# The sums of the up-projection's weights: made on GpSimd in the mLSTM heads, kept in DRAM, loaded as weight tiles

## The chip, the core and the metric

The program runs on one core of one Trainium2 chip. The metric is device time in microseconds (us), the median of several executions. The engines are named as in the profile: PE is TensorE (matmuls), PEld its weight loads, DVE is VectorE, ACT is ScalarE, POOL is GpSimd, and SP is SyncE, whose queue issues the DMAs of this kernel. Each engine, SP too, takes its instructions strictly in the order in which the program has them.

## What is computed

One layer of a decoder in float32, for 1024 prompt rows and 8 × 8 sample rows: an input projection, four retention heads and four mLSTM heads, an output projection, and a feed-forward part with a causal convolution of width 3:

```python
h = rmsnorm(x, pre_mix_g)
proj = (h @ w_in).astype(f32)                       # 1024 -> 4 x 512 + 4 x 512 + 8
ret_out, S_new = retention_chunked(q_r, k_r, v_r, S_ret)
ml_out, C_new, n_new, m_new = mlstm_chunked(q_m, k_m * scale, v_m, i_pre, f_pre, C, n, m)
...
x = x + rmsnorm(mix, post_mix_g)
h2 = rmsnorm(x, pre_ffn_g)
up = h2 @ w_up                                      # 1024 -> 2 x 2816
padded = jnp.concatenate([conv_buf, up], axis=1)
conv = sum(padded[:, j:j + L] * conv_w[j] for j in range(CONV_W)) + conv_b
gate, val = conv[..., :D_FF], conv[..., D_FF:]
ffn = (gelu(gate) * val) @ w_down                   # 2816 -> 1024
x = x + rmsnorm(ffn, post_ffn_g)
```

## The kernel before

**Products.** Every float32 operand of a matmul is split into a high and a low part (ACT copies the high part, DVE subtracts it from the operand to get the low one, `split_to`, L145 and L147), and each product is three matmuls: high × high, high × low, low × high. The 1088 rows stand in four blocks of 272 columns, so that a matmul of the projections is 128 × 128 weights on 272 columns.

**Stages.** Loads and the first norm (to about 50 us of the profiled execution); the retention heads r0 to r3 (to 295); the mLSTM heads m0 to m3 (to 515); the output projection (to about 650); the norm behind it, together with the first two column tiles of the up-projection in plain form (`PLAIN` = 2; to 712); the other 20 column tiles j = 2 to 21 (to about 1152); the down-projection and the last norm.

**A head** (`mix_head`, L468) has five turns (L662): two pairs of 128-row chunks, the sample rows, two more pairs. Before each turn `front` projects the inputs of the next one. The weights `st_in` are loaded by SP (L133, two buffers) and split. For the sample rows GpSimd makes `vx` (L613) and scales the old state `sb` by `dec` (L616, mLSTM heads only); PE multiplies `vx` (`us`, L621), DVE adds (L624), and the state is stored (L627) and the next head's loaded into the same single buffer (L502). On GpSimd there is nothing else in the mLSTM heads. At the end of each turn `next(rows, None)` takes one step of a generator, which is in use during the retention heads alone.

**The up-projection.** A column tile j is a pair of 128 columns, one of the gate and one of the value. Its four 128 × 512 weight blocks A11, A12, A21, A22 (the inner dimension in two halves, gate and value) are not multiplied as they are: with sums of them (Strassen's scheme, in Winograd's form) there are seven products of half the inner dimension for two blocks of rows instead of eight. `weight_prep(j)` loads two 512 KB tiles `st_up` (L133), GpSimd makes the four sums in place (L859, L865 to L867: 128 × 512 each), and seven halves of 128 × 512 are split one at a time on ACT and DVE. A j has 7 products × 2 row blocks × 12 matmuls = 168 matmuls (L928 to L930); DVE adds what comes out of PSUM (L902, L906), and DVE and ACT make the convolution (L941, L943, L948), GELU and the product of the two (L950), GpSimd the sums of those for the down-projection (L958).

**Order.** The Tile framework orders the instructions of each engine ahead of time with a model of their durations; the result is one fixed list for each engine. All DMAs stand in SP's one list. A DMA that waits for its data (a store that waits for GpSimd) holds up all that stand behind it there.

**Memory.** `tok` (L226) hands out 128 × 1088 tiles in turn from seven buffers; two of them are taken at the start by the rotary tables `rot`, which are last used in the retention heads.

Of the kernel before, what the change touches and what calls it, by code (L numbers as in the profile page):

```python
# [23 lines left out]
T = LP + TS  # L24
# [7 lines left out]
JT = DFF // P  # L32
# [5 lines left out]
PLAIN = 2  # L38
# [54 lines left out]
def hybrid_layer_kernel(ctx: ExitStack, tc: tile.TileContext, a: dict, o: dict):  # L93
    nc = tc.nc
# [9 lines left out]
    last = {}  # L104
# [4 lines left out]
    dr = pool("dr", bufs=1, space=bass.MemoryType.DRAM)  # L109
# [21 lines left out]
    def stage_w(src, name):  # L131
        st = wp.tile([P, 2 * HB], F32, tag="wst", name=f"st_{name}")[:, :D]
        nc.sync.dma_start(st, src)  # L133
        return st
# [7 lines left out]
    def split_to(x, hi, lo, eng=nc.vector, after=None):  # L142
        act, dve = after or (None, None)
        with tc.issue_after(act.ins) if act else nullcontext():
            nc.scalar.activation(hi, x, AF.Copy)  # L145
        with tc.issue_after(dve.ins) if dve and eng is nc.vector else nullcontext():
            eng.tensor_tensor(lo, x, hi.bitcast(F32), ALU.subtract)  # L147
        return hi, lo
# [69 lines left out]
    mpool = lambda name, **k: mixctx.enter_context(tc.tile_pool(name=name, **k))  # L218
    mp = mpool("mp", bufs=1)
    cst = mp.tile([P, C_N], F32, name="cst")  # L220
    rb = mp.tile([P, T], F32, name="rb")
    ident = cst[:, C_ID:C_ID + P]
    tokp = mpool("tokp", bufs=7)
    m2 = mpool("m2", bufs=2)

    def tok(name, rows=P, dt=F32):  # L226
        return tokp.tile([P, T], dt, tag="tok", name=name)[:rows, :]
# [1 line left out]

    h = []  # L230
    xs = [flat("x", b, k=KT) for b in range(4)]
    rot = [tok(f"rot{i}") for i in range(2)]
    nc.sync.dma_start(vec, a["vec"])
    first = (2 * NH, 2 * NH + 1)
    staged = [stage_w(a["wi"][first[0]], f"in{first[0]}")]
# [12 lines left out]
    sums = [m2.tile([P, NB, 129], F32, tag=t, bufs=1, name=f"sums_{t}").rearrange("p s v -> p (s v)") for t in ("vx", "sb")]  # L248
    sqs = [m2.tile([P, Q], F32, tag="sw", name=f"sq{i}") for i in range(2)]
    for b in range(4):  # L250
        n = BLK[b][1]
# [57 lines left out]
    cols = mp.tile([P, 9, 3 * NH], F32, name="cols")  # L309
# [158 lines left out]
    def mix_head(hd, ml):  # L468
# [207 lines left out]
        nc.sync.dma_start(o["cp" if ml else "sp"][hd], S)  # L676
        todo()

    rows = iter(())
    for hd in range(NH):  # L680
        mix_head(hd, False)
        if hd == 0:
            gate_proj()
            rows = gate_rows()
    for _ in rows:
        pass
    for hd in range(NH):
        mix_head(hd, True)

    mx = []  # L690

# [28 lines left out]
    fp = pool("fp", bufs=2)  # L720
# [4 lines left out]
    def wtile():  # L725

        wtag[0] += 1
        return (wp, "w") if wtag[0] % 4 in (1, 2) else (fp, "d")
# [102 lines left out]
    acc = out_proj(0)  # L831
    acc = out_proj(1, spaced(post_mix(0, acc)))
    acc = out_proj(2, spaced(post_mix(1, acc)) + [lambda: first_half(0)])
    acc = out_proj(3, spaced(post_mix(2, acc)) + [lambda: first_half(1)])
# [5 lines left out]

    def weight_prep(j):

        h0, h1 = slice(0, D // 2), slice(D // 2, D)
        s0, s1 = stage_w(a["wu"][j, 0], f"up{j}_0"), stage_w(a["wu"][j, 1], f"up{j}_1")
        a11, a12, a22, a21 = s0[:, h0], s0[:, h1], s1[:, h0], s1[:, h1]
        plain = j < PLAIN
        t1 = None if plain else fp.tile([P, D // 2], F32, tag="s1", bufs=1, name=f"s1_{j}")
        ws = {}

        def parts(i, eng=nc.vector, **src):  # L850
            p, tag = wtile()
            hi = p.tile([P, D], F32R, tag=tag + "hi", name=f"wh_up{j}_{i}")
            lo = p.tile([P, D], F32R, tag=tag + "lo", name=f"wl_up{j}_{i}")
            for (name, x), c in zip(src.items(), (h0, h1)):
                ws[name] = split_to(x, hi[:, c], lo[:, c], eng, (last["sq"], last["acc"]) if i in (1, 2) else None)

        e = nc.gpsimd
        if not plain:
            e.tensor_tensor(t1, a21, a22, ALU.add)  # L859
        parts(0, A11=a11, A12=a12)  # L860
        if plain:
            parts(3, A22=a22, A21=a21)
            yield ws
            return
        e.tensor_tensor(a21, a11, a21, ALU.subtract)  # L865
        e.tensor_tensor(a11, t1, a11, ALU.subtract)  # L866
        e.tensor_tensor(a12, a12, a11, ALU.subtract)  # L867
        yield ws
        parts(1, S2=a11, S1=t1)
        yield  # L870
        parts(2, S4=a12, S3=a21)
        yield
        parts(3, A22=a22)
        yield

    def half(U, th, i):
# [101 lines left out]
    sums = {"T1": mo[0][0], "T3": mo[0][1], "T2": mo[1][1]}  # L978
    firsts = []

    def begin_plain(j):
        ws = next(weight_prep(j))
        firsts.append((j, ws, up_products(j, ws)[1]()))
# [139 lines left out]
    acc = [t_acc[b // 2][:, b % 2 * Q:(b % 2 + 1) * Q] for b in range(4)]  # L1123
# [172 lines left out]
```

## Time and profile before

| | before |
|---|---|
| median of 3 runs | 1428.85 us (1427.64 to 1430.25) |
| the profiled execution, own time | 1428.44 us |
| its span from first to last instruction | 1426.7 us |
| PE busy | 1361.6 us (95%) |
| DVE busy | 1060.2 us (74%) |
| ACT busy | 587.0 us (41%) |
| POOL busy | 436.4 us (31%) |
| bytes moved by DMA | 135.12 MB, 95 GB/s over the span |
| mean granted TensorE clock | 0.985 of full speed |

The busy time of an engine is the time in which one of its instructions ran, waits left out. PE is busy nearly everywhere, so the first question to each part of the kernel is how many of its matmuls ran in how much time; the matmuls' own durations overlap (a matmul of 272 columns is shown with some 290 ns, while they follow each other every 125 ns).

### The profile page before, as it was taken

The page shows a single profiled execution, that of the slowest core. Times are in us where ns is not written, and L with a number is a line of the kernel's source. Part 1 is how long each engine was busy: PE and PEld are TensorE (multiplying, and loading weights), DVE is VectorE, ACT ScalarE, POOL GpSimd, SP SyncE. Part 2 cuts the span into 40 slices and gives each one's busy share as a digit, 9 for nine tenths or more (in the row PEclk, how much of TensorE's full clock was granted, in tenths as well). Part 3 has the DMA queues.
Part 4 walks back from the last instruction along what each step waited for, and adds up shares of the span by engine and source line. Part 5 has one row for each costly group of instructions (what it writes and reads, how often), then busy time and mean ns, then how long its engine had stood idle before and what let it go on. Part 6 is the DMA issues. An engine that isn't in the chain of part 4 may idle for free. (4 is left out here: it accounts for less than half of the span.)

```text
span 1426.7 us, 26779 instructions
## 1 busy us (share of the span) xinstructions
PE 1361.6 (95%) x10575; PEld 1332.3 (93%) x10575; DVE 1060.2 (74%) x2064; ACT 587.0 (41%) x1162; POOL 436.4 (31%) x433
## 2 busy tenths in 40 slices
PE   7999999999999999999998999999999979999993
PEld 7899999999999998999998999999999979999993
DVE  7845875455455466568899999999989995995577
ACT  6423542323223236445553433433433444454462
POOL 5200000001001000004456466465465460952015
PEclk9999999999999999999999999999999989999997
DMA  6112111121121113323022223322223394333352
GB/s 233 60 45 73 41 59 54 53 62 48 45 62 47 45 47 112 113 63 122 32 92 87 89 88 112 107 85 84 99 85 115 116 404 121 95 91 93 97 197 114
DMA packets 64478, 135.12 MB, mean 95 GB/s; under 512 B 6112, under 2 KB 30688, under 8 KB 63840
## 3 DMA queue, kind: packets, MB, share of 16 engines
q1 hardware_dynamic: 64352, 133.41, 27.6%
q8 instruction: 83, 1.36, 0.4%
q14 instruction: 43, 0.35, 0.1%
HBM read 97.88 MB, written 35.50 MB: 93 GB/s over the span
## 5 line engine op out<-in xcount | busy, mean ns | idle before, releaser
L159 PE MATMUL in<-hh,wh_in 128*128 128x272 f32 x1024 | 301.8, 295 | 11.1 <-ACT hh L198 6.8
L161 PE MATMUL in<-hh,wl_in 128*128 128x272 f32 x1024 | 301.1, 294 | 1.1 <-DVE wl_in L147 1.1
L160 PE MATMUL in<-hl,wh_in 128*128 128x272 f32 x1024 | 299.8, 293 | 1.2 <-DVE hl L199 1.2
L159 PEld LDWEIGHTS in<-hh,wh_in 128*128 128x128 f32 x1024 | 195.4, 191 | 12.9 <-ACT hh L198 6.8
L161 PEld LDWEIGHTS in<-hh,wl_in 128*128 128x128 f32 x1024 | 194.9, 190 | 3.7 <-issue 2.1
L160 PEld LDWEIGHTS in<-hl,wh_in 128*128 128x128 f32 x1024 | 195.4, 191 | 2.4 <-DVE hl L199 1.5
L147 DVE TENSOR_TENSOR wl_up<-st_up,wh_up 128x512 fp32r<-128x512 f32 x128 | 125.4, 985 | 9.5 <-ACT wh_up L145 9.4
L145 ACT ACTIVATE wh_up<-st_up 128x512 fp32r<-128x512 f32 x128 | 75.1, 620 | 133.1 <-POOL st_up L866 120.4
L1054 DVE TENSOR_TENSOR rb<-rb 128x544 fp32r<-128x544 f32 x78 | 73.1, 949 | 42.4 <-ACT rb L1053 42.2
L943 DVE SCALAR_TENSOR_TENSOR c<-Ug,vec,c 128x1024 f32<-128x1024 f32 x88 | 79.4, 939 | 9.5 <-ACT c L941 9.5
L1074 POOL TENSOR_TENSOR wd<-wd 128x512 f32<-128x512 f32 x44 | 72.0, 1667 | 42.7 <-DVE ra_dhi L1054 33.1
L943 DVE SCALAR_TENSOR_TENSOR c<-Uv,vec,c 128x1024 f32<-128x1024 f32 (+1 forms) x88 | 71.9, 822 | 9.3 <-ACT c L941 9.3
L958 POOL TENSOR_TENSOR act<-act 128x544 f32<-128x544 f32 x44 | 72.4, 1645 | 14.7 <-DVE act L950 10.3
L1053 ACT ACTIVATE rb<-rb 128x544 fp32r<-128x544 f32 x78 | 49.8, 648 | 64.3 <-DMA rb<-bd 58.4
L613 POOL TENSOR_TENSOR vx_r<-vts,cst 64x1024 f32<-64x1024 f32 x4 | 7.6, 1901 | 191.8 <-ACT vts L527 191.8
L902 DVE TENSOR_TENSOR Uv<-Uv,up_S 128x272 f32<-128x272 f32 (+1 forms) x200 | 63.5, 369 | 0.0
L941 ACT ACTIVATE c<-Ug,vec 128x1024 f32<-128x1024 f32 (+1 forms) x44 | 34.6, 835 | 67.0 <-DVE Ug L906 59.3
L145 ACT ACTIVATE wh_in<-st_in 128x1024 fp32r<-128x1024 f32 x32 | 33.9, 1059 | 62.3 <-PE in L160 58.3
L893 POOL MEMSET Ug<- 128x2 f32 x22 | 2.2, 100 | 176.9 <-DVE xr L791 82.1
L859 POOL TENSOR_TENSOR s<-st_up 128x512 f32<-128x512 f32 x20 | 29.0, 1450 | 85.2 <-DMA st_up<-in_wu 82.1
L613 POOL TENSOR_TENSOR vx_m<-vts,cst 64x1032 f32<-64x1032 f32 x4 | 7.7, 1914 | 152.6 <-DVE pt_m L559 152.6
L928 PE MATMUL up_A<-T4h,wh_up 128*128 128x272 f32 x160 | 47.9, 299 | 4.8 <-DVE Uv L902 4.7
(547 smaller groups left out, 4825.1 us busy)
## 6 DMA issues: line engine op xcount, KB each, us to landing
st_up<-in_wu SPq DMA_DIRECT2D x44, 512.0 KB, 3.3
rb<-bd SPq DMA_DIRECT2D x76, 272.0 KB, 2.8
bd<-act SPq DMA_DIRECT2D x33, 544.0 KB, 2.7
st_in<-in_wi SPq DMA_DIRECT2D x32, 512.0 KB, 3.3
wd<-in_wd SPq DMA_DIRECT2D x22, 512.0 KB, 9.3
x<-in_x SPq DMA_DIRECT2D x16, 272.0 KB, 7.0
xr<-in_x SPq DMA_DIRECT2D x8, 544.0 KB, 3.7
x1d<-mo SPq DMA_DIRECT2D x8, 544.0 KB, 3.1
```

The lines of the kernel that those rows point to most:

```text
L145: nc.scalar.activation(hi, x, AF.Copy)
L147: eng.tensor_tensor(lo, x, hi.bitcast(F32), ALU.subtract)
L159: nc.tensor.matmul(ps, hi[:, ws], xh, start=k == 0, stop=False)
L160: nc.tensor.matmul(ps, hi[:, ws], xl, start=False, stop=False)
L161: nc.tensor.matmul(ps, lo[:, ws], xh, start=False, stop=k == KT - 1)
L902: nc.vector.tensor_tensor(o_, o_ if x is None else c(x), c(ps), ALU.add)
L928: nc.tensor.matmul(ps, wh[:, c], xh[:, k, n], start=k == 0, stop=False)
L943: nc.vector.scalar_tensor_tensor(c, u(i), cw(i), c, ALU.mult, ALU.add)
L958: nc.gpsimd.tensor_tensor(o_, x, y, ALU.subtract)
L1053: nc.scalar.activation(hi, x, AF.Copy)
L1054: nc.vector.tensor_tensor(lo, x, hi.bitcast(F32), ALU.subtract)
L1074: nc.gpsimd.tensor_tensor(quad(p, out), quad(p, x), quad(p, y), op)
```

## The change

For j = 2 to 21 the sums of the weights are no longer made in the up-projection. During the four mLSTM heads a new generator `weight_sums` takes the weights in 40 pieces: two pieces c = 0, 1 for each j, one j for each of the 5 × 4 turns. For a piece SP loads 256 columns of each of the four blocks in two DMAs of 256 KB (128 × 2 × 256 elements each), GpSimd makes the four sums in place (128 × 256 each), and SP stores the 512 KB tile with S2, S1, S4, S3 to a tensor `sd` in DRAM. In the up-projection `weight_prep` then loads, for each j, the 512 KB tile of A11 and A12, two 512 KB tiles from `sd`, and the 256 KB of A22 alone; it splits three times 128 × 1024 and once 128 × 512, in place of seven times 128 × 512, and GpSimd makes no sums there.

The pieces lie in the two tiles that held `rot` (one buffer for each c); for that, `rot` has tiles of its own, and `tok` has five buffers in place of seven.

```diff
-    tokp = mpool("tokp", bufs=7)
+    tokp = mpool("tokp", bufs=5)
...
-    rot = [tok(f"rot{i}") for i in range(2)]
+    rot = [mp.tile([P, T], F32, tag=f"rot{i}", name=f"rot{i}") for i in range(2)]
...
+    sd = dr.tile([JT, P, 4, D // 2], F32, name="sd")
+
+    def weight_sums():
+
+        for j in range(PLAIN, JT):
+            for c in range(2):
+                cols = slice(c * 256, c * 256 + 256)
+                g = mp.tile([P, T], F32, tag=f"rot{c}", name=f"sg{j}_{c}")[:, :D].rearrange("p (b n) -> p b n", b=4)
+                w0, w1 = (a["wu"][j, q].rearrange("p (b n) -> p b n", b=2)[:, :, cols] for q in range(2))
+                nc.sync.dma_start(g[:, 1:3, :], w0)
+                nc.sync.dma_start(g[:, 0::3, :], w1)
+                a22, a11, a12, a21 = (g[:, i, :] for i in range(4))
+                for o_, x, y, op in ((a21, a11, a21, ALU.subtract), (a22, a22, a21, ALU.subtract),
+                                     (a11, a22, a11, ALU.add), (a12, a12, a22, ALU.subtract)):
+                    nc.gpsimd.tensor_tensor(o_, x, y, op)
+                nc.sync.dma_start(sd[j][:, :, cols], g)
+                if c:
+                    yield
+
...
+    rows = weight_sums()
     for hd in range(NH):
         mix_head(hd, True)
+    for _ in rows:
+        pass
...
-        h0, h1 = slice(0, D // 2), slice(D // 2, D)
-        s0, s1 = stage_w(a["wu"][j, 0], f"up{j}_0"), stage_w(a["wu"][j, 1], f"up{j}_1")
-        a11, a12, a22, a21 = s0[:, h0], s0[:, h1], s1[:, h0], s1[:, h1]
...
-        def parts(i, eng=nc.vector, **src):
+        def parts(i, x, *names):
             p, tag = wtile()
-            hi = p.tile([P, D], F32R, tag=tag + "hi", name=f"wh_up{j}_{i}")
-            lo = p.tile([P, D], F32R, tag=tag + "lo", name=f"wl_up{j}_{i}")
-            for (name, x), c in zip(src.items(), (h0, h1)):
-                ws[name] = split_to(x, hi[:, c], lo[:, c], eng, (last["sq"], last["acc"]) if i in (1, 2) else None)
+            n = len(names) * D // 2
+            hi = p.tile([P, D], F32R, tag=tag + "hi", name=f"wh_up{j}_{i}")[:, :n]
+            lo = p.tile([P, D], F32R, tag=tag + "lo", name=f"wl_up{j}_{i}")[:, :n]
+            split_to(x, hi, lo, nc.vector, (last["sq"], last["acc"]) if i in (1, 2) else None)
+            for c, name in enumerate(names):
+                cols = slice(c * D // 2, (c + 1) * D // 2)
+                ws[name] = hi[:, cols], lo[:, cols]
...
-        if not plain:
-            e.tensor_tensor(t1, a21, a22, ALU.add)
-        parts(0, A11=a11, A12=a12)
+        parts(0, stage_w(a["wu"][j, 0], f"up{j}_0"), "A11", "A12")
...
-        e.tensor_tensor(a21, a11, a21, ALU.subtract)
-        e.tensor_tensor(a11, t1, a11, ALU.subtract)
-        e.tensor_tensor(a12, a12, a11, ALU.subtract)
         yield ws
-        parts(1, S2=a11, S1=t1)
-        yield
-        parts(2, S4=a12, S3=a21)
-        yield
-        parts(3, A22=a22)
+        sums = sd[j].rearrange("p b n -> p (b n)")
+        for i, names in ((1, ("S2", "S1")), (2, ("S4", "S3"))):
+            parts(i, stage_w(sums[:, (i - 1) * D:i * D], f"up{j}_{i}"), *names)
+            yield
+        st = fp.tile([P, D // 2], F32, tag="s1", bufs=1, name=f"st_up{j}_3")
+        nc.sync.dma_start(st, a["wu"][j, 1][:, :D // 2])
+        parts(3, st, "A22")
         yield
```

Lines below the diff's first part carry new numbers in the changed kernel: the loads of `weight_sums` are L689 and L690, its sums L694, its store L695; L902 becomes L920, and L943 becomes L961. In rows of the order a DMA is shown with the shape of one side, and the number at the end of a name is the buffer's.

Where the order changes, first on SP, at the passage from head r3 to m0 (`st_in` are weights of the input projection, `out_ss` the store of a retention state, `sb` the load of the next state, `sg` the pieces). Before:

```order
L133 DMA st_in24_3672<-in_wi 128x1024
L133 DMA st_in17_4103<-in_wi 128x1024
L627 DMA out_ss<-sb_r3_3174 1024x1x128
L502 DMA sb_m0_3782<-in_sc 128x8x128
L133 DMA st_in21_4213<-in_wi 128x1024
```

The same place in the changed kernel:

```order
L133 DMA st_in17_4184<-in_wi 128x1024
L689 DMA sg3_1_3921<-in_wu 128x2x256
L690 DMA sg3_1_3921<-in_wu 128x2x256
L695 DMA sd_276<-sg3_0_3913 512x1x256
L689 DMA sg4_0_4015<-in_wu 128x2x256
L695 DMA sd_276<-sg3_1_3921 512x1x256
L690 DMA sg4_0_4015<-in_wu 128x2x256
L627 DMA out_ss<-sb_r3_3175 1024x1x128
L689 DMA sg4_1_4023<-in_wu 128x2x256
L690 DMA sg4_1_4023<-in_wu 128x2x256
L502 DMA sb_m0_3783<-in_sc 128x8x128
L695 DMA sd_276<-sg4_0_4015 512x1x256
```

So loads and stores of the pieces stand between the loads that the heads need, and each store waits in that list for GpSimd. On GpSimd, the sample rows of head m0, before:

```order
L506 COPY sb_m0_3782<-sn_m0_3784 128x8
L613 TENSOR_TENSOR vx_m0_3938<-vts1_267,cst_81 64x1032
L616 TENSOR_TENSOR sb_m0_3782<-sb_m0_3782,dec_m0_3787 128x1032
L629 COPY sn_m0_3784<-sb_m0_3782 128x8
L506 COPY sb_m1_4433<-sn_m1_4435 128x8
```

And there in the changed kernel:

```order
L694 TENSOR_TENSOR sg7_0_4590<-sg7_0_4590 128x256 x4
L694 TENSOR_TENSOR sg7_1_4598<-sg7_1_4598 128x256 x4
L613 TENSOR_TENSOR vx_m0_3971<-vts1_267,cst_81 64x1032
L694 TENSOR_TENSOR sg8_0_4644<-sg8_0_4644 128x256 x2
L694 TENSOR_TENSOR sg8_1_4652<-sg8_1_4652 128x256
L694 TENSOR_TENSOR sg8_0_4644<-sg8_0_4644 128x256 x2
L694 TENSOR_TENSOR sg8_1_4652<-sg8_1_4652 128x256
L616 TENSOR_TENSOR sb_m0_3783<-sb_m0_3783,dec_m0_3788 128x1032
L694 TENSOR_TENSOR sg8_1_4652<-sg8_1_4652 128x256 x2
L629 COPY sn_m0_3785<-sb_m0_3783 128x8
```

`vx` of m0 now stands behind all sums up to j = 7, and each of these waits for its piece's loads. The third place is DVE in the up-projection, tile j = 15 (`up15_...` are products in PSUM, `c3` the convolution, `wl_up16` low parts of the next tile's weights). Before:

```order
L902 TENSOR_TENSOR Uv15_11666<-Uv15_11666,up15_S31_11847 128x208
L902 TENSOR_TENSOR Uv15_11666<-Uv15_11666,up15_S31_11847 128x8x8
L902 TENSOR_TENSOR Uv15_11666<-Uv15_11666,up15_S31_11847 128x272
L147 TENSOR_TENSOR wl_up16_2_11864<-st_up16_0_11725,wh_up16_2_11863 128x512
L943 SCALAR_TENSOR_TENSOR c3_8292<-Ug15_11663,vec_67,c3_8292 128x1024
L943 SCALAR_TENSOR_TENSOR c3_8292<-Ug15_11663,vec_67,c3_8292 128x64
L147 TENSOR_TENSOR wl_up16_2_11864<-st_up16_1_11727,wh_up16_2_11863 128x512
L902 TENSOR_TENSOR Uv15_11666<-Uv15_11666,up15_A220_11869 128x272
```

In the changed kernel:

```order
L920 TENSOR_TENSOR Uv15_11881<-Uv15_11881,up15_S31_12053 128x208
L920 TENSOR_TENSOR Uv15_11881<-Uv15_11881,up15_S31_12053 128x8x8
L920 TENSOR_TENSOR Uv15_11881<-Uv15_11881,up15_S31_12053 128x272
L961 SCALAR_TENSOR_TENSOR c3_8598<-Ug15_11878,vec_67,c3_8598 128x1024
L961 SCALAR_TENSOR_TENSOR c3_8598<-Ug15_11878,vec_67,c3_8598 128x64
L147 TENSOR_TENSOR wl_up16_2_12072<-st_up16_2_12069,wh_up16_2_12071 128x1024
L920 TENSOR_TENSOR Uv15_11881<-Uv15_11881,up15_A220_12075 128x272
```

Two splits of 512 columns around the convolution have become one of 1024 behind it; the evacuations and the convolution keep their places. The order on PE is the same but for some matmuls of head m1.

More of the change, by code (lines that the diff above doesn't have):

```diff
@@ L841, in weight_prep @@
     def weight_prep(j):
-        h0, h1 = slice(0, D // 2), slice(D // 2, D)
-        s0, s1 = stage_w(a["wu"][j, 0], f"up{j}_0"), stage_w(a["wu"][j, 1], f"up{j}_1")
-        a11, a12, a22, a21 = s0[:, h0], s0[:, h1], s1[:, h0], s1[:, h1]
         plain = j < PLAIN
-        t1 = None if plain else fp.tile([P, D // 2], F32, tag="s1", bufs=1, name=f"s1_{j}")
         ws = {}
-        def parts(i, eng=nc.vector, **src):
+        def parts(i, x, *names):
             p, tag = wtile()
-            hi = p.tile([P, D], F32R, tag=tag + "hi", name=f"wh_up{j}_{i}")
-            lo = p.tile([P, D], F32R, tag=tag + "lo", name=f"wl_up{j}_{i}")
-            for (name, x), c in zip(src.items(), (h0, h1)):
-                ws[name] = split_to(x, hi[:, c], lo[:, c], eng, (last["sq"], last["acc"]) if i in (1, 2) else None)
-        e = nc.gpsimd
-        if not plain:
-            e.tensor_tensor(t1, a21, a22, ALU.add)
-        parts(0, A11=a11, A12=a12)
+            n = len(names) * D // 2
[6 more added lines that the diff above has]
+        parts(0, stage_w(a["wu"][j, 0], f"up{j}_0"), "A11", "A12")
         if plain:
-            parts(3, A22=a22, A21=a21)
+            parts(3, stage_w(a["wu"][j, 1], f"up{j}_1"), "A22", "A21")
             yield ws
             return
-        e.tensor_tensor(a21, a11, a21, ALU.subtract)
-        e.tensor_tensor(a11, t1, a11, ALU.subtract)
-        e.tensor_tensor(a12, a12, a11, ALU.subtract)
         yield ws
-        parts(1, S2=a11, S1=t1)
-        yield
-        parts(2, S4=a12, S3=a21)
-        yield
-        parts(3, A22=a22)
+        sums = sd[j].rearrange("p b n -> p (b n)")
[5 more added lines that the diff above has]
+        parts(3, st, "A22")
         yield
```

## Prediction

> **What bounds the kernel now.** First the head of the page: is one engine the bound, and at what clock?
>
> ```profile
> span 1426.7 us, 26779 instructions
> PE 1361.6 (95%) x10575; PEld 1332.3 (93%) x10575; DVE 1060.2 (74%) x2064; ACT 587.0 (41%) x1162; POOL 436.4 (31%) x433
> ...
> PE   7999999999999999999998999999999979999993
> ...
> PEclk9999999999999999999999999999999989999997
> ```
>
> PE is busy in nearly every slice, at 95% of the span, at full clock; the whole remainder is 65 us. So a change that leaves the matmuls alone can only win PE's gaps, and the question is which gaps lie in the two stages that it touches. Next the windows, one for the mLSTM heads, two for the up-projection, one for the down-projection as a yardstick (columns: window, length, busy us and instructions of PE, PEld, DVE, ACT, POOL, then clock, DMA share, GB/s):
>
> ```profile
> 290.00:515.00 225.00, 225.00 (x1788) 216.38 (x1787) 115.44 (x424) 59.33 (x173) 16.86 (x16) 1.00 0.17 52
> 700.00:825.00 125.00, 118.63 (x928) 116.63 (x927) 120.62 (x174) 58.82 (x95) 75.53 (x81) 1.00 0.23 81
> 825.00:1125.00 300.00, 296.79 (x2339) 294.14 (x2338) 277.13 (x457) 121.11 (x195) 166.83 (x195) 1.00 0.26 94
> 1325.00:1350.00 25.00, 25.00 (x202) 25.00 (x201) 15.68 (x28) 10.98 (x19) 0.00 (x0) 1.00 0.34 95
> ```
>
> In the last window matmuls follow one another without a gap: 202 with two cut by its edges, 200 in 25 us, 0.125 us each. By that step the up-projection's windows have matmuls for 928 × 0.125 = 116.0 us of 125 (9.0 lost) and 2339 × 0.125 = 292.4 us of 300 (7.6 lost). DVE is at 96% and 92% there. In the mLSTM heads PE is busy in all of 225 us, and DVE in half of it.
>
> A second count, over all 20 tiles, from the first matmul of product A11 to its last:
>
> ```profile
> L928 PE MATMUL up_A<-B1h,wh_up x160: 283/288/365, 712.3 to 1131.8; 128*128 128x272 f32 x160
> ```
>
> Between 712.3 and 1131.8 lie 19 tiles × 168 matmuls and 21 of the 20th, 3213 × 0.125 = 401.6 us of 419.5: **17.9 us lost**. That is all that this stage has to give. Who loses it, the waits between 715 and 1145 us say (us in total, times, longest):
>
> ```profile
> ACT wh_up L145 <- POOL st_up L866: 120.4, 17, 7.9
> ...
> PEld up_A L928 <- DVE Uv L902: 5.9, 14, 0.7
> ...
> PE up_A L928 <- DVE Uv L902: 4.6, 11, 1.6
> ...
> PE up_S L928 <- DVE Uv L902: 3.5, 5, 1.3
> ```
>
> PE waits for L902, DVE's evacuation of an earlier product, since a new product needs its PSUM bank; it hardly waits for weights. ACT's 120 us wait for GpSimd's sums is cover, not loss: the split weights are still in time. So the loss is DVE's, a nearly full engine with a list that now and then runs late.
>
> **The gain in the up-projection.** DVE's work is made smaller in two ways. What the splits cost now, and what a split twice as wide costs:
>
> ```profile
> L147 DVE TENSOR_TENSOR wl_up<-st_up,wh_up 128x512 fp32r<-128x512 f32 x128 | 125.4, 985 | 9.5 <-ACT wh_up L145 9.4
> L147 DVE TENSOR_TENSOR wl_up<-s,wh_up 128x512 fp32r<-128x512 f32 x20 | 32.0, 1601 | 0.0
> L147 DVE TENSOR_TENSOR wl_in<-st_in,wh_in 128x1024 fp32r<-128x1024 f32 x32 | 39.6, 1237 | 11.9 <-ACT wh_in L145 11.5
> ...
> L147 DVE TENSOR_TENSOR wl_up<-st_up,wh_up x128: 674/683/1779, 647.5 to 1138.4; 128x512 fp32r<-128x512 f32 x128
> ```
>
> Of seven splits a tile has six of the first row and one of the second: 6 × 0.985 + 1.601 = 7.5 us. After the change there are three of 1024 at 1.237 us (third row) and one of 512 at its undisturbed median of 0.683: 4.4 us. **3.1 us a tile** less. A tile takes 419.5 us / (3213 / 168) = 21.9 us, so DVE falls from 92% to (0.92 × 21.9 − 3.1) / 21.9 = 78%.
>
> Why the mean is 0.985 where the median is 0.683: DVE is held by GpSimd. The clearest case lies in the mLSTM heads (timeline: start, duration; then the same line's durations):
>
> ```profile
> 342.15 1.91 POOL L616 TENSOR_TENSOR sb_m<-sb_m,dec_m 128x1032 f32<-128x1032 f32 x1 [4.52 <-PE o_m L608]
> 342.56 1.50 DVE L578 SCALAR_TENSOR_TENSOR den_m0s<-on_m0s 64x1 f32<-64x1 f32 x1
> ...
> L578 DVE SCALAR_TENSOR_TENSOR den_m<-on_m x8: 146/148/149, 339.7 to 515.9; 128x4 f32<-128x4 f32 x8
> ...
> L902 DVE TENSOR_TENSOR Uv<-Uv,up_A x40: 421/426/434, 742.6 to 1164.3; 128x272 f32<-128x272 f32 x40
> ```
>
> An operation of 0.15 us takes 1.50 us and ends with GpSimd's, 344.06 us both. L902, which takes one input from PSUM, is never longer than 0.434 us though GpSimd is busy in half of that stage. So only DVE operations with two SBUF inputs are held; the splits are such, and the sums are what holds them. GpSimd still has L958 and L1074 there, so some holding stays.
>
> Of the 17.9 us I take **13**: nearly all of the second window's 7.6, where a DVE that is 78% full can catch up, and some 5.5 of the rest, where two more conv outputs and the operand sums of the start compete for DVE whatever the weights do. Bounds: 0 (the order of evacuations on DVE is the same, and the wait is set by order, not by load) and 17.9.
>
> The Trainium skill, page "Perfetto Trace Analysis", section "Identifying the Most-Contended Engine", says to judge TensorE's headroom by the weight loads' busy share rather than the matmuls'; here PEld has 294.14 of 300 us, 5.9 lost in place of 7.6, and by it the forecast would be some 2 us later.
>
> ACT goes from 7 halves to 3 wide splits and one half and is far from full; SP has four loads a tile in place of two, 1.75 MB in place of 1 MB in 21.9 us, about 34 GB/s more on 94. The third load comes a product pair ahead of its use by the order, and lands in some 3.3 us: I cost both at nothing. Without that cover a tile would lose about one landing time, 3 us.
>
> **The cost in the mLSTM heads: GpSimd holds DVE.** The sums' price, from the nearest width:
>
> ```profile
> L205 POOL TENSOR_TENSOR sq<-x x28: 636/832/1691, 6.0 to 48.8; 128x272 f32<-128x272 f32 x28
> ...
> L859 POOL TENSOR_TENSOR s<-st_up x20: 1282/1369/2220, 670.0 to 1120.8; 128x512 f32<-128x512 f32 x20
> ```
>
> Undisturbed, 272 columns take 0.636 us and 512 take 1.282, so 256 take some 0.62; I take 0.65, since DVE is half idle here (high end: the median of the crowded first stage, 0.83). 160 × 0.65 = 104 us, in some 240 us: GpSimd is in a sum 43% of the time. A finish of a head's group has seven small DVE operations with two SBUF inputs, of which L578 is one (8 + 4 finishes: 84), and 12 splits of `st_in` come to it: 96. One that comes while a sum runs waits half of it: 96 × 0.43 × 0.32 = 13 us on DVE. DVE is idle half of this stage, and PE waits for nothing in it; only where DVE works without pause, after the sample rows, does this reach PE. I take **3 us**, bounds 0 and 13.
>
> The Trainium skill ("SBUF — State Buffer", "Who interferes with whom") calls this an exclusive lock that the loser waits out entirely; the 1.50 us row agrees with it, and it speaks against moving sums beside the heads. Its exception for operations with one SBUF input is borne out by L902.
>
> **The cost in the mLSTM heads: the loop of a piece.** A piece's buffer is loaded, summed, stored, and only then free. What the trace has for such DMAs (KB each, us to landing):
>
> ```profile
> st_in<-in_wi SPq DMA_DIRECT2D x32, 512.0 KB, 3.3
> ...
> x1d<-mo SPq DMA_DIRECT2D x8, 544.0 KB, 3.1
> ...
> sb_m<-in_sc SPq DMA_DIRECT2D x4, 512.0 KB, 4.2
> out_cs<-sb_m SPq DMA_DIRECT2D x4, 512.0 KB, 3.9
> rb<-bd SPq DMA_DIRECT2D x76, 272.0 KB, 2.8
> ```
>
> Two loads of 256 KB side by side are taken at 3.1 (272 KB: 2.8; 512 KB: 3.3 to 4.2), the store at 3.2 (3.1 to 3.9), the four sums at 2.6, handing over at 0.3: **9.2 us** a loop, at most 4.2 + 3.9 + 4 × 0.83 + 0.3 = 11.7. The time that it has, one turn:
>
> ```profile
> L613 POOL TENSOR_TENSOR vx_m<-vts,cst x4: 1912/1914/1916, 335.7 to 494.9; 64x1032 f32<-64x1032 f32 x4
> ...
> 335.71 1.92 POOL L613 TENSOR_TENSOR vx_m<-vts,cst 64x1032 f32<-64x1032 f32 x1 [39.89 <-DVE pt_m L559]
> ...
> 341.94 1.60 PEld L621 LDWEIGHTS us_m<-vx_m,kz_m 64*128 64x128 f32 x6 [0.17 <-issue]
> ```
>
> (494.9 − 335.7) / 3 / 5 = 10.6 us a turn, of which I leave 0.6 for SP's and GpSimd's other entries: 10. Two buffers run at once, and GpSimd's sums of both, 5.2 us, fit into it. With 9.2 the loop keeps up, `vx` comes in time, and the term is 0. If it fell behind, `vx` (in GpSimd's list behind all sums up to j = 7) would have 341.94 − 337.63 = 4.3 us before PE stands. The 40 stores that wait in SP's list can delay the weights behind them; GpSimd waits 39.9 us ahead of `vx` today, and weights come a whole projection ahead, so this too is 0 as long as the loop keeps up.
>
> **Elsewhere.** `tok` with five buffers and `rot` on its own leave the retention heads the five that they had. The mLSTM heads have five for seven; the order on PE is the same, so 0. The turn to the down-projection at 1140 to 1180 us moves forward as it is.
>
> **Sum.** 1428.4 − 13 + 3 = 1418.4 us for the profiled execution, which is 0.4 under the median of the runs: **1419 us**. Differences within 0.2% (2.9 us) are about what a measurement of this kernel cannot tell from no change.
>
> **The rivals.**
>
> *The loop is too slow* (slower): at C us a loop, 20 turns lose C − 10 each, less the 4.3 us of slack, at `us` on PE behind a late `vx`. For it: sums, loads and stores are chained through one SP list, and 0.8 us is the whole margin. Against it: the rows' middle values give 9.2. At C = 10.7 it eats the 10 us of net gain; at 11.7 it costs 30 us and the kernel takes 1449. Chance 0.20, most of it on the slower side.
>
> *The order on DVE, not its load, makes PE wait* (same): evacuations now stand behind a split of 1.2 us where they stood behind one of 0.68, and the conv operations of 0.9 us stay. For it: PE's single waits are short, up to 1.6 us, as one operation ahead in a list would make them. Against it: DVE at 96% where the loss is larger, 92% where it is smaller. About 4 us would come back: 1428.4 − 4 + 3, on the median 1428. Chance 0.13.
>
> *The whole loss comes back and holding costs nothing*: 1428.4 − 17.9, on the median 1411. Chance 0.05.
>
> **The numbers.** Forecast (1413 to 1424) 0.62. Faster: 0.62 + 0.05 + 0.03 of the second and third rival's edges = 0.70; within 0.2%: 0.12; slower: 0.18. The range goes from the full gain, 1411, to 1434, a loop of about 11 us; it leaves out some 0.15, above.
>
> **What would show it.** The count of matmuls: a tile every 21.2 to 21.4 us in place of 21.9. DVE at some 78% in 825 to 1125 us, wide splits near 1.24 us, PE's waits for L902 (now L920) down by more than half. In the heads: `vx` still 53.0 us apart, and no idle time of PE ahead of `us`; if PE stands there, the loop was too slow and I was wrong on the price of a loop. Small DVE operations of 0.15 us drawn out to 0.3 to 0.75 us in the heads show the holding; if it shows as idle PE of more than 13 us there, that term was wrong. If DVE falls to 78% and PE's waits stay, the second rival was right.

## The result, and the profile after

The changed kernel takes **1448.41 us** (median of 4 runs, 1444.32 to 1450.48) where the one before takes 1428.76: a ratio of 1.0133, 95% interval 1.0109 to 1.0157. It is slower by some 20 us, outside the range given. Its profiled execution has a span of 1446.2 us, 19.5 more than before. The head of its page:

```profile
span 1446.2 us, 26997 instructions
PE 1366.2 (94%) x10575; PEld 1338.0 (93%) x10575; DVE 1010.8 (70%) x2000; ACT 586.6 (41%) x1098; POOL 420.7 (29%) x513
...
PEclk9999999998989898999999999999999999999997
```

The number of matmuls is the same, DVE is busy 49 us less, and yet the time is longer. Four slices of the clock row, all in the mLSTM heads, are down by a tenth; before there were none there. Cut at the first and the last A11 product of the 20 tiles (the row of the first product, here for the changed kernel), the span falls into three parts:

```profile
L946 PE MATMUL up_A<-B1h,wh_up x160: 283/288/291, 756.7 to 1159.9; 128*128 128x272 f32 x160
```

| us | to the first A11 | the 20 tiles | from the last A11 to the end |
|---|---|---|---|
| before | 712.3 | 419.5 | 294.9 |
| changed | 756.7 | 403.2 | 286.3 |
| difference | +44.4 | −16.3 | −8.6 |

So the up-projection did what the change wanted, and better than forecast: 403.2 us for matmuls of 401.6, and DVE down to 79% in this window (237.54 of 300 us), PE without a gap:

```profile
840.00:1140.00 300.00, 300.00 (x2393) 300.00 (x2392) 237.54 (x429) 124.69 (x159) 73.48 (x142) 1.00 0.41 134
```

The 44.4 us come from the heads. The line of `vx` in the changed kernel:

```profile
L613 POOL TENSOR_TENSOR vx_m<-vts,cst x4: 1904/1906/1909, 344.9 to 539.8; 64x1032 f32<-64x1032 f32 x4
```

PE's waits from 270 to 560 us (us in total, times, longest):

```profile
PE us_m L621 <- POOL vx_m L613: 24.2, 4, 10.2
PE s_m L557 <- DVE sb_m L624: 4.9, 2, 3.9
```

`vx` comes 9.2 us late in m0 and 44.9 us late in m3, 65.0 us apart where it was 53.0. PE, which in this window waited 1.3 us before, all of it at the output projection behind the heads, now stands 29.1 us. That is less than 44.4. The rest is the clock, seen first in the windows around the first such wait (after the five engines: granted clock, DMA share, GB/s):

```profile
335.00:345.00 10.00, 4.89 (x41) 4.30 (x40) 8.58 (x32) 2.33 (x9) 5.80 (x9) 1.00 0.74 243
345.00:350.00 5.00, 3.10 (x5) 1.82 (x6) 2.00 (x3) 0.61 (x3) 1.85 (x1) 0.51 0.72 211
350.00:355.00 5.00, 5.00 (x21) 4.37 (x20) 0.00 (x0) 0.00 (x0) 3.67 (x6) 0.50 0.31 104
355.00:360.00 5.00, 4.00 (x34) 3.79 (x33) 2.40 (x9) 1.21 (x3) 4.03 (x5) 0.97 0.36 119
```

PE stands from about 340 to 347 us, and then works at half clock until about 355: 21 matmuls in 5 us where 40 would fit. A wait of 7 us has so cost some 11. In windows of 0.5 us from 270 to 560 us, PE was busy for 35.1 us at a granted clock near 0.5 (none before); the half of it that is lost, some 17 us, with the 29.1 us of waits makes the 44.4 within 3 us. The Trainium skill, page "TensorE: Matmul & The Clock Gate", Part 1 on the clock gate, says that an idle window halves the clock and that sustained work releases it; the granted clock of 0.50 after the wait agrees.

Why `vx` is late, the chain that ends at `vx` of m0 shows (start, duration, what):

```profile
326.95 2.41 POOL sg L694 x2
...
329.38 3.23 DMA sd<-sg
...
332.62 0.54 SPq L689
...
333.27 0.56 SPq L695
...
333.88 4.85 DMA sg<-in_wu
...
338.89 0.73 POOL sg L694
```

Nothing but the loop of the pieces: sums, store, the next load, sums, up to `vx`. Within it stands a foreign entry, L695 at 333.27: between the two loads of a piece, SP issues the *other* piece's store. What the parts cost, first from the page's DMA issues (KB each, us to landing), then from the lines of a piece's two loads and of the sums:

```profile
sg<-in_wu SPq DMA_DIRECT2D x80, 256.0 KB, 3.4
sd<-sg SPq DMA_DIRECT2D x40, 512.0 KB, 4.1
```

```profile
L689 SPq DMA_DIRECT2D sg<-in_wu x40: 539/540/638, 265.3 to 528.9; - x40
...
DMA to landing us min/median/max: 3.0/3.3/5.7
```

```profile
L690 SPq DMA_DIRECT2D sg<-in_wu x40: 600/624/991, 265.9 to 530.2; - x40
...
DMA to landing us min/median/max: 3.2/4.2/6.0
```

```profile
L694 POOL TENSOR_TENSOR sg<-sg x160: 713/733/1722, 270.9 to 539.1; 128x256 f32<-128x256 f32 x160
```

And what SP waited for in the heads:

```profile
SPq L689 <- DMA sd<-sg: 97.5, 37, 5.6
SPq L695 <- POOL sg L694: 59.6, 21, 4.9
```

The 3.4 us of the page is the median of both loads together; the sums wait for the second one (L690), which lands in 4.2. So: the issue of the first load, behind which the second one stands, 0.6; the second one's landing 4.2; handing over 0.3, an estimate; four sums 3.1 (4 × the mean of 0.784); store 4.1. That makes 12.3 us, where 9.2 was taken and 11.7 was the high end. (The expectation for the stores on ACT's queue below counts 3.4 and so has 11.5.) And the loop in fact took more: the list has six tiles ahead of `vx` of m0, begun at 265.3 and done at 344.9, **13.3 us a tile**. To be in time at 335.7 it would have needed 11.7.

### The profile page after: what moved, and what is told of

It reads as the page before. It is cut to its first block, busy times and chain, and to the rows that moved or that the text cites. A ratio compares the mean times of both kernels' runs of the same rounds, so it can differ in the third digit from the quotient of the medians.

```text
span 1446.2 us, 26997 instructions
## 1 busy us (share of the span) xinstructions
PE 1366.2 (94%) x10575; PEld 1338.0 (93%) x10575; DVE 1010.8 (70%) x2000; ACT 586.6 (41%) x1098; POOL 420.7 (29%) x513
## 4 chain that ended last, share of the span: by engine, by line
PE 67%; DMA 13%; DVE 8%; POOL 4%; issue 3%; ACT 2%; SPq 1%; DVEq 0%; POOLq 0%; ACTq 0%
DMA sd<-sg 6%; DMA sg<-in_wu 5%; PE up_S L948 5%; PE up_S L947 5%; PE up_S L946 5%; PE in L161 5%; PE in L159 5%; PE in L160 5%; PE dn L1137 4%; PE dn L1138 4%; PE dn L1136 4%; PE up_A L947 4%; PE up_A L946 4%; PE up_A L948 4%; POOL sg L694 4%
## 5 line engine op out<-in xcount | busy, mean ns | idle before, releaser
L159 PE MATMUL in<-hh,wh_in 128*128 128x272 f32 x1024 | 304.9, 298 | 10.4 <-ACT hh L198 6.0
L161 PE MATMUL in<-hh,wl_in 128*128 128x272 f32 x1024 | 304.6, 298 | 0.9 <-DVE wl_in L147 0.9
L161 PEld LDWEIGHTS in<-hh,wl_in 128*128 128x128 f32 x1024 | 198.3, 194 | 4.7 <-issue 3.4
L694 POOL TENSOR_TENSOR sg<-sg 128x256 f32<-128x256 f32 x160 | 123.1, 784 | 170.3 <-DMA sg<-in_wu 164.4
L145 ACT ACTIVATE wh_up<-st_up 128x1024 fp32r<-128x1024 f32 x84 | 80.5, 958 | 164.5 <-PE up_S L947 98.9
L147 DVE TENSOR_TENSOR wl_up<-st_up,wh_up 128x1024 fp32r<-128x1024 f32 x84 | 96.9, 1154 | 8.4 <-ACT wh_up L145 8.4
L920 DVE TENSOR_TENSOR Uv<-Uv,up_S 128x272 f32<-128x272 f32 (+1 forms) x200 | 66.8, 377 | 45.8 <-PE up_S L948 45.8
L976 POOL TENSOR_TENSOR act<-act 128x544 f32<-128x544 f32 x44 | 69.1, 1571 | 67.3 <-DMA bd<-act 34.5
L961 DVE SCALAR_TENSOR_TENSOR c<-Uv,vec,c 128x1024 f32<-128x1024 f32 (+1 forms) x88 | 72.2, 824 | 8.6 <-ACT c L959 8.6
L961 DVE SCALAR_TENSOR_TENSOR c<-Ug,vec,c 128x1024 f32<-128x1024 f32 x88 | 68.7, 820 | 1.4 <-ACT c L959 1.4
L147 DVE TENSOR_TENSOR wl_in<-st_in,wh_in 128x1024 fp32r<-128x1024 f32 x32 | 43.1, 1346 | 10.3 <-ACT wh_in L145 9.9
L1213 POOL TENSOR_TENSOR facc<-facc,x1r 128x816 f32<-128x816 f32 (+1 forms) x10 | 21.4, 2158 | 91.0 <-DVE facc L1212 85.1
```

Of the source, the lines that this page charges most:

```text
L159: nc.tensor.matmul(ps, hi[:, ws], xh, start=k == 0, stop=False)
L161: nc.tensor.matmul(ps, lo[:, ws], xh, start=False, stop=k == KT - 1)
L694: nc.gpsimd.tensor_tensor(o_, x, y, op)
L961: nc.vector.scalar_tensor_tensor(c, u(i), cw(i), c, ALU.mult, ALU.add)
```

## The experiments

Theory L: the loop's lateness, carried into the heads by `vx`, is the loss. Rivals: H, GpSimd's sums hold DVE; T, the missing token buffers. The table after the experiments has the three parts of every kernel's profiled execution. Where only one time is given, it is a single run; the kernel before, run beside them, took 1425.7 to 1430.7 us.

**The up-projection alone.** `weight_sums` isn't stepped, and the tiles of sums are raw blocks:

```diff
-    rows = weight_sums()
+    rows = iter(())
...
-            parts(i, stage_w(sums[:, (i - 1) * D:i * D], f"up{j}_{i}"), *names)
+            parts(i, stage_w(a["wu"][j, i - 1], f"up{j}_{i}"), *names)
```

> The sums are not made at all: the heads run without the pieces, and the up-projection loads raw weight blocks of the same size in the place of the stored sums, so its result is another one. Every theory: the heads are as before (vx_m 53.0 us apart), the 20 tiles lose 1.6 us in place of 17.9. If the 8.6 us that the changed kernel is faster behind the up-projection come from the lighter up-projection: 1404 us. If they come from the shifted heads: 1412 us.

1403.28 us, 24.7 less than the kernel before beside it: 16.4 us in the 20 tiles and 8.6 behind them. Both belong to the lighter up-projection; the sum of the two, some 25 us, is the change's whole possible gain.

**The heads alone**: the loop as changed, the up-projection as before (`weight_prep` of before put back).

> The pieces are loaded, summed and stored in the heads, but the up-projection is that of before with its own sums. Both theories: first matmul of A11 some 44 us late as in the changed kernel. If the up-projection's gain is 16.3 us and the 8.6 us behind it belong to it as well: 1473 us. If the 8.6 us belong to the shifted heads: 1464 us.

1469.05 us, between the two times expected; the parts decide. To the first A11 753.6 us (+41.3), then 419.2 and 294.2, as before within 0.7: the 8.6 us belong to the up-projection. The two halves of the change are nearly independent: +41 and −25 make 16, and the changed kernel is 19.5 us longer.

**No store** (and the up-projection again loads raw blocks):

```diff
-                nc.sync.dma_start(sd[j][:, :, cols], g)
```

> Loads and sums of all pieces as in the changed kernel, but no store; the up-projection loads raw blocks in the place of the sums, so its result is another one. Theory L (the loop of a piece, load, sums, store through the one list of SP, takes 13 us where a turn has 10.6): without the store a piece needs 1.1 + 3.3 + 3.1 + 0.3 = 7.8 us, vx_m is in time again, and the time is that of up_only plus 0 to 5 us. Rival H (160 sums on GpSimd hold DVE and push vx back): the sums are all there, so vx_m stays some 12 us late a head, and the time is within 10 us of the changed kernel's 1448.

1424.12 us: outside both theories' ranges. Without the store the loop is faster, but `vx` of m0 is as late as ever:

```profile
L613 POOL TENSOR_TENSOR vx_m<-vts,cst x4: 1908/1910/1914, 345.4 to 515.5; 64x1032 f32<-64x1032 f32 x4
```

The order tells why. With a shorter loop the planner's model puts more into the list: 9 tiles stand ahead of `vx` of m0 (6 in the changed kernel) and 16 ahead of m1's (11). From 267.3 to 345.4 that is 8.7 us a tile, which it was to do in 7.6. So theory L needs a correction: not the loop's length against a turn decides, but its length against what the planner's model made of it when it wrote the list. The list is filled as early as the model allows, and each tile that runs longer than modelled pushes `vx` back. Call this L2. The model's own durations are not on record: 7.6 here, and 11.7 in the changed kernel, are the time up to `vx` of before, shared out over the tiles ahead of it.

**Room alone**: five token buffers, `rot` on its own, no more.

```diff
-    tokp = mpool("tokp", bufs=7)
+    tokp = mpool("tokp", bufs=5)
...
-    rot = [tok(f"rot{i}") for i in range(2)]
+    rot = [mp.tile([P, T], F32, tag=f"rot{i}", name=f"rot{i}") for i in range(2)]
```

> The kernel before with five token buffers and the rotary tables in tiles of their own, nothing else. L and H: 1428.8 us within 3. Rival T (the mLSTM heads wait for token buffers): vx_m late by some us a head, over 1433 us.

1429.81 us, `vx` at its times of before (335.3 to 494.4). T is out.

**Twelve tiles**: a step of `weight_sums` only in three of five turns, sums ahead for j = 2 to 13; the other eight tiles are summed in the up-projection as before.

```diff
+    AHEAD = range(PLAIN, PLAIN + 12)
...
-        for j in range(PLAIN, JT):
+        for j in AHEAD:
...
-            next(rows, None)
+            if not ml or i in (0, 1, 3):
+                next(rows, None)
```

> Sums ahead for 12 of the 20 tiles only, three turns of each mLSTM head, the other 8 tiles as before. If the load on a turn decides (17.7 us a tile are then there for a loop of 13 us): no late vx, 12/20 of the 25 us that up_only gained, 1414 us. Theory L2: the list still has 6 tiles ahead of vx_m0 and 11 ahead of vx_m1, since the planner takes them as early as its model allows; the first two heads are as late as in the changed kernel (some 20 us), the last two in time: 1432 to 1438 us.

1430.04 us, 2 us under L2's range and 16 over the other one; to the first A11 +23.5. As L2 says: giving a tile more turns doesn't slow the list, which again has 6 and 11 tiles ahead of the first two `vx`; PE waits for `vx` twice, and not in the last two heads:

```profile
PE us_m L621 <- POOL vx_m L613: 13.7, 2, 7.6
```

**Stores on ACT's queue**:

```diff
-                nc.sync.dma_start(sd[j][:, :, cols], g)
+                nc.scalar.dma_start(sd[j][:, :, cols], g)
```

> The changed kernel with the 40 stores issued by ACT's queue instead of SP's, so that a store that waits for GpSimd does not hold up the other piece's loads. If this coupling in SP's list makes up the difference between the parts of a loop (0.6 + 3.4 + 0.3 + 3.1 + 4.1 = 11.5 us) and the 13.3 us seen: the loop takes some 11.5 us, vx_m0 is in time, and the time is 1410 to 1430 us. If the coupling is not what matters: 13 us, vx_m0 9 us late, within 10 us of 1448.

1430.56 us. The time is at the edge of one range, the mechanism is not its own: the loop only went to some 12.8 us a tile (517.8 − 267.3 us from the first load of the first piece to that of the last, 39 pieces on, two a tile; 13.5 so counted in the changed kernel), `vx` of m0 is still 8.9 us late, and ACT now waits for sums with a head's own work behind. PE's waits for `vx` are 0.9 us in all; it stands 20.8 us from 270 to 535 us, mostly for what DVE and ACT make. The 0.7 us less a tile is what the stores' landing alone can account for (3.4 us at the median, 4.1 before); that the other piece's store in SP's list costs anything is not shown.

**`vx`, the scaling of `sb` and the two copies on DVE** in the mLSTM heads, and the same in the kernel before as a control:

```diff
-            nc.gpsimd.tensor_tensor(vx, vt[:TS, 0, :W].unsqueeze(1).broadcast_to([TS, NB, W]),
+            (nc.vector if ml else nc.gpsimd).tensor_tensor(vx, vt[:TS, 0, :W].unsqueeze(1).broadcast_to([TS, NB, W]),
...
-                nc.gpsimd.tensor_tensor(sb, sb, dec[:, 8:16].unsqueeze(2).broadcast_to([P, NB, W]), ALU.mult)
+                nc.vector.tensor_tensor(sb, sb, dec[:, 8:16].unsqueeze(2).broadcast_to([P, NB, W]), ALU.mult)
```

> The changed kernel, but in the mLSTM heads vx, the scaling of sb and the two small copies are made by DVE instead of GpSimd, so that nothing that a head needs stands behind a sum. Theory L2 (PE waits because vx stands in GpSimd's fixed list behind as many pieces as the planner's model thought would be done by then, 6 tiles for m0, and the real loop takes 13.3 us a tile where the list allows 11.7): the loop stays as slow, its sums end near 265 + 20 x 13 = 525 us, but vx_m comes every 53 to 54 us, PE waits for us_m vanish, and the time is that of up_only, 1403 us, plus 0 to 8 us. Rival H (the sums slow the heads by holding DVE, or the traffic slows the weights): the heads stay late, over 1420 us.

> The kernel before with vx, the scaling of sb and the two copies of the mLSTM heads on DVE, and no piece at all. Both theories: 1428.8 us within 3, since DVE is idle half of that stage; if it is slower by more, the same loss is in vx_on_dve.

The control is 1429.6 us, no change. The changed kernel with it: 1436.24 us (ratio 1.0067, 1.0050 to 1.0085); 12 us better, not the 1403 to 1411 expected, and by the time alone an outcome for H. The waits for `us` are gone, and others stand in their place:

```profile
PE yt_m0s L594 <- DVE on_m0s L592: 8.3, 1, 8.3
PE yt_m2s L594 <- DVE on_m2s L592: 8.2, 1, 8.2
...
DVE sb_m L506 <- DMA out_cs<-sb_m: 18.8, 2, 9.9
DVE sb_m L506 <- DMA out_ns<-sn_m: 11.8, 1, 11.8
```

DVE stands, in order, at a write to `sb`, whose old state must first be stored (L627); SP issues the first such store at 357.5 us, behind two pieces' stores that waited for GpSimd. So there are **two** lists that carry the loop's lateness into the heads, GpSimd's and SP's.

**Own queue**: also the pieces' DMAs issued by GpSimd, so that nothing of a head stands behind a piece anywhere.

```diff
-                nc.sync.dma_start(g[:, 1:3, :], w0)
-                nc.sync.dma_start(g[:, 0::3, :], w1)
+                nc.gpsimd.dma_start(g[:, 1:3, :], w0)
+                nc.gpsimd.dma_start(g[:, 0::3, :], w1)
...
-                nc.sync.dma_start(sd[j][:, :, cols], g)
+                nc.gpsimd.dma_start(sd[j][:, :, cols], g)
```

> Like vx_on_dve, and the loads and stores of the pieces are issued by GpSimd itself, so that neither GpSimd's nor SP's list makes a head wait for a piece. Theory L3 (two lists carry the loop's lateness into the heads: GpSimd's, with vx behind sums, and SP's, with the next state's load and weights behind stores): no wait of PE in the heads above 2 us, the heads 53 to 54 us apart; the sums end at 530 to 550 us, which the start of the output projection may wait for. Time 1403 to 1415 us. If the heads stay late though nothing stands behind a piece, it is holding or traffic: over 1420 us.

> The pieces' DMAs issued by GpSimd, but vx and the scaling of sb on GpSimd as in the changed kernel. L3: SP's list is free, GpSimd's is not, so vx is late by as much as or more than in the changed kernel (the waits for DMAs now stand in GpSimd's list): 1440 to 1470 us. Rival (SP's list was the whole cause): below 1420 us.

> Like own_queue, for 16 of the 20 tiles; the last four are summed in the up-projection as before. If the end of the sums holds up the output projection in own_queue, this one starts it in time and loses 4/20 of the 16.3 us of the up-projection and perhaps the 8 us at the turn to the down-projection: 1406 to 1415 us. If not, it is 3 to 11 us slower than own_queue.

With `vx` on DVE and the own queue: 1417.67 us, ratio 0.9927 (0.9905 to 0.9948), just above what was expected, and faster than before; the heads are nearly in time with the sums and DMAs beside them, which speaks against H. `vx` comes at 335.1 to 498.0 us, 3.1 late in m3. The sums end late, and the output projection waits for that (the sums' line; PE's waits):

```profile
L694 POOL TENSOR_TENSOR sg<-sg x160: 714/737/1762, 273.1 to 568.2; 128x256 f32<-128x256 f32 x160
```

```profile
PE out L159 <- ACT wh_out L145: 3.9, 1, 3.9
```

Some 9 of the 12.6 us to the first A11 lie there: from 503 us on PE stands 14.3 us (8.0 in the kernel before from 500 on) and loses 4.3 to the clock (1.7).

With `vx` left on GpSimd: 1437.59 us, just under its range, `vx` up to 17.6 us late and again the late end, at 586 us; so SP's list was not the whole cause. PE's waits for `vx` are only 4.0 us of that, and some 20 of the 33.4 us to the first A11 lie behind the heads. With 16 tiles, whose sums end at 507 us:

```profile
L613 DVE TENSOR_TENSOR vx_m<-vts,cst x4: 1226/1752/2398, 333.7 to 499.9; 64x1032 f32<-64x1032 f32 x4
...
L975 PE MATMUL up_A<-B1h,wh_up x160: 283/288/291, 716.0 to 1119.2; 128*128 128x272 f32 x160
```

**1411.04 us, ratio 0.9877 (0.9848 to 0.9905)**: the best of those that compute the layer, and faster than both kernels. H is weighed by it too: 128 of the 160 sums run beside the heads, with their traffic, and the first A11 is 3.7 us late, 1.2 of which the control without pieces has as well. That holds everything which these sums and DMAs cost the heads apart from the lists.

**What in the up-projection won the 25 us?** Once the sums away with seven narrow splits of raw halves, once the sums left and the splits made wide (S2 with S4, and A22 with S3, which lie side by side after the sums). The second one's edit:

```diff
-        parts(1, S2=a11, S1=t1)
+        parts(1, s0, "S2", "S4")
+        parts(2, t1, "S1")
...
-        parts(3, A22=a22)
+        parts(3, s1, "A22", "S3")
```

> The kernel before without GpSimd's four sums a tile in the up-projection: the raw halves are split, seven narrow ones a tile as before, so its result is another one. If the gain comes from GpSimd being out of the way (splits at 0.68 us in place of 0.985 and 1.60, and the sums of the activations and their stores earlier at the turn to the down-projection): 1403 to 1407 us. If it comes from the wide splits: 1420 us or more.

> The kernel before with its sums on GpSimd in the up-projection, but three wide splits and one narrow a tile (S2 with S4 and A22 with S3, which lie side by side). If GpSimd is what matters: the splits stay held (1.3 us or more for a wide one), the turn to the down-projection stays, 1418 to 1429 us. If the number and width of the splits matter: 1403 to 1410 us.

Without sums, 1402.74 us: 403.2 us for the tiles, the whole gain, with narrow splits whose mean fell from 0.985 (and 1.60 for S1) to 0.764 us. It leaves the sums out and so computes another result. With wide splits, 1417.19 us, a little under its expected range: 408.6 us for the tiles, but 294.9 behind them as before. The splits of the two:

```profile
L147 DVE TENSOR_TENSOR wl_up<-st_up,wh_up 128x512 fp32r<-128x512 f32 x148 | 111.0, 764 | 2.3 <-ACT wh_up L145 0.3
```

```profile
L147 DVE TENSOR_TENSOR wl_up<-st_up,wh_up 128x1024 fp32r<-128x1024 f32 x64 | 92.8, 1450 | 35.1 <-ACT wh_up L145 35.1
```

Either way of relieving DVE brings back most of the tiles' loss. What lies behind the tiles is won only where GpSimd makes fewer sums in the tiles. It is PE's standing and the clock: in the 70 us after the last A11, PE stands 10.1 us before and 6.1 in the changed kernel, and the granted clock takes 5.1 and 1.7 (busy time times the missing share of the clock, in windows of 0.5 us). In the kernel before, from 1100 to 1150 us, SP's store of the activations waited for GpSimd's sums of activations (L958), which stood among the weights' sums, and the loads of the down-projection behind it in SP's list:

```profile
SPq L960 <- POOL act L958: 8.3, 2, 4.5
```

The first of those loads is issued 5.7 us after the last A11 in the kernel before, 5.8 in heads_only and 3.4 in wide_with_sums, the three with 294 to 295 us behind the tiles. It is issued 0.4 to 0.5 us after it in the changed kernel, up_only, sums_out_narrow, own_queue and own_queue_16, which have 283 to 290. That own_queue_16 is among these, though its last four tiles are summed as before, says that the sums of the earlier tiles matter too.

**Early sums**: `own_queue_16` with the four summed tiles first instead of last.

```diff
-    AHEAD = range(PLAIN, PLAIN + 16)
+    AHEAD = range(JT - 16, JT)
```

> own_queue_16 with the four tiles that are summed in the up-projection at its front (j = 2 to 5) instead of its end. If GpSimd's sums of the last tile hold up the stores at the turn to the down-projection: from the last tile's first product to the end 286 to 287 us in place of own_queue_16's 290 (as in up_only, 286.3), so some 3.5 us faster, 1406 to 1409 us. If the 8.6 us have another source: 1411 us within 2.

1417.81 us (ratio 0.9931, 0.9913 to 0.9948), over both times expected and slower than with the sums at the end. Behind the tiles only 1.2 us are won (288.7 against 289.9; kernels whose up-projection is that of before differ there by up to 1.6), but the tiles take 411.9 us in place of 403.2: sums cost much among the first tiles, and nothing in the last four. So the last tile's sums are not the whole 8.6 us. That these come with the sums leaving GpSimd is shown (up_only and sums_out_narrow against wide_with_sums); most of them go with the earlier issue of the down-projection's loads, but how they divide between that and DVE's backlog at the end stays open.

The parts add up to the span of the profiled execution, which is not always the median one (in own_queue 1413.20 us, 4.5 under it).

| us | to the first A11 | the 20 tiles | behind | median or single time |
|---|---|---|---|---|
| up_only | 712.1 | 403.1 | 286.3 | 1403.28 |
| heads_only | 753.6 | 419.2 | 294.2 | 1469.05 |
| loop_without_store | 733.0 | 403.1 | 285.8 | 1424.12 |
| room_only | 713.3 | 418.9 | 295.8 | 1429.81 |
| twelve_tiles | 735.8 | 403.2 | 289.3 | 1430.04 |
| stores_on_act | 741.0 | 403.2 | 284.1 | 1430.56 |
| vx_on_dve | 743.5 | 403.2 | 285.3 | 1436.24 |
| before_vx_on_dve | 713.5 | 419.5 | 294.7 | 1429.60 |
| own_queue_vx_on_gpsimd | 745.7 | 403.2 | 286.9 | 1437.59 |
| own_queue | 724.9 | 403.1 | 283.4 | 1417.67 |
| own_queue_16 | 716.0 | 403.2 | 289.9 | 1411.04 |
| sums_early_16 | 714.9 | 411.9 | 288.7 | 1417.81 |
| sums_out_narrow | 709.5 | 403.2 | 287.9 | 1402.74 |
| wide_with_sums | 711.9 | 408.6 | 294.9 | 1417.19 |

## Why the prediction was wrong

- **The step that failed is the loop of a piece**: "With 9.2 the loop keeps up, `vx` comes in time, and the term is 0." Its parts came to 12.3 us and the loop to 13.3, `vx` was 9.2 us late in m0, and the term measured +44.4 us in place of 0. Each part was taken near the low end of its rows: the store 3.2 (4.1 measured; rows 3.1 to 3.9), four sums 2.6 (3.1), the two loads side by side 3.1 (4.2 for the second, and 0.6 for the issue ahead of it, which had no time at all). Small optimisms in one chain, with 0.8 us of margin, were no basis for a 0. `sb` and `out_cs`, the strided transfers of the very stage, were the nearer rows, and gave the high end of 11.7.
- **And the chain was held to be two independent buffers.** The order in the document shows the other piece's store between a piece's two loads; it was read as a danger for the weights, not as a part of the loop. Whether the 1.0 us between 12.3 and 13.3 lies there stays open; stores_on_act didn't show it. The stores in SP's list were put at 0 "as long as the loop keeps up"; it didn't, and with `vx` out of GpSimd's list (vx_on_dve) the first A11 is still 31.2 us late.
- **The rival named the mechanism**, `us` on PE behind a late `vx`, at 1449 us for a loop of 11.7, against 1448.41 measured. That number is partly luck: it was a price of 20 × 1.7 − 4.3 = 30 us with a PE at full clock. Measured are 29.1 us of waits and some 15 more from a clock at half, which the price left out; the gain against it was larger than forecast; and the wait did not come turn by turn, but from what stood ahead of `vx` in the list. With 0.8 us as "the whole margin", 0.20 was a low chance.
- **The slack was read against the turn** (10.6 us, "I leave 0.6"). GpSimd's list has the pieces as early as the planner put them, so slack in the turns doesn't help `vx`: twelve tiles, with 17.7 us each, were late by as much in the first two heads (10.4 and 23.5 us, against 9.2 and 24.6). What counts, by these lists, is how far a tile's time exceeds what was planned for it, times the tiles that the list has ahead.
- **The gain was mis-sized, the mechanism right**: 13 of 17.9 us were taken, 16.3 came (DVE at 79%, forecast 78%). The second rival (order, not load) is out: the order stayed and the waits went.
- **"The turn to the down-projection … moves forward as it is"** was wrong by 8.6 us, in the kernel's favour, so that even the low bound of 1411 was not one: the up-projection alone gives 1403.
- **Holding of DVE in the heads** was taken at 3 us; own_queue_16, at 128 sums, is 3.7 late in all, and sums_early_16 2.6. The term's size is borne out; no run isolates the holding.
- The token buffers at 0: right (room_only).

## What to carry to other kernels

Work moved into idle time of an engine is free only if nothing that another engine waits for stands behind it, in any in-order list that it touches: the engine's own, and the DMA queue's. Where a planner writes the list from a model, look at how much stands ahead of the critical instruction and what an error of 14% in its durations (13.3 us for 11.7 here) would do. Here the critical instruction on another engine, a queue of its own for the new work, and 16 of the 20 tiles came out 17 us faster than before instead of 20 slower. And a chain of load, work and store is priced from the slow rows of that stage, with every issue in it.

## What the hardware showed that was not expected

- A wait of PE costs more than its length: after some 7 us without matmuls the granted clock was 0.50 for about 8 us more. In the heads 29.1 us of waits came with a delay of 44.4, and PE was busy at half clock for 35.1 us.
- DMAs issued by GpSimd were not slower as a whole in the heads: an issue takes 0.72 us (0.54 to 0.62 on SP), in own_queue the loads landed in 4.4 us at the median (3.4 from SP's queue) and the stores in 3.4 (4.1).
- Two fifths more transfer in the up-projection were free: 134 GB/s in place of 94, with PE busy in all of the 300 us.
